# Moving one head's share of the attention output ahead of the block products

## The chip, the cores and the metric

The kernel runs on one core of a Trainium2 chip. Its engines run side by side, each with its own queue of instructions: PE multiplies matrices into PSUM, DVE and ACT do elementwise work (DVE on two tensors, ACT casts, copies and functions), POOL does a little elementwise work and issues some DMAs, SP issues most DMAs. The metric is device time in microseconds from the start to the end of one execution, lower is better.

## The reference

One layer of a decoder trunk on a sequence of 1024 tokens with 1024 features: a mixer of three head groups, then cross-attention into 256 memory tokens, then a gated feed-forward layer. The change is in the cross-attention and its seam to the feed-forward layer. Cut to that:

```python
def cross_attention(hn, mn, w_xq, w_xkv, w_xo):      # 4 heads of 256
    q = (hn @ w_xq).reshape(Bsz, S, N_XHEADS, DH_X)
    k, v = ...                                       # from mn @ w_xkv, 256 memory tokens
    s = jnp.einsum('bshd,bmhd->bhsm', q, k).astype(jnp.float32) * (DH_X ** -0.5)
    p = jax.nn.softmax(s, axis=-1).astype(v.dtype)
    o = jnp.einsum('bhsm,bmhd->bshd', p, v).reshape(Bsz, S, D_MODEL)
    return o @ w_xo

h = h + cross_attention(rmsnorm(h, norm_x_g), rmsnorm(mem, norm_mem_g), w_xq, w_xkv, w_xo)
h = h + conv_glu(rmsnorm(h, norm_ffn_g), w_up, conv_f_w, conv_f_b, w_down)
```

## The kernel before

**Precision.** Every float32 operand is split into a high and a low half (`split`: ACT casts the high half, DVE subtracts it to get the low one), and a product is three matmuls, high x high, high x low and low x high (`mm3`).

**Blocks and order.** The tokens are two blocks of 512, `b` = 0 and 1; the stream lies transposed as `h[b]`, eight tiles `n` of 128 features by 512 tokens. A planner writes out each engine's order from the place of an instruction in the program, with its own estimates of durations; a `high_priority` block sets an earlier place for what stands in it. On the chip each engine follows its written order and waits where an operand is not there yet. Tiles come from pools with a fixed number of places for each tag; a tile waits until a place is free. `big` has six places of 16 KB a partition (tag `b16`). Pools that are opened after others were closed lie on the memory of those, so what is written there waits for the last readers of what lay there.

**Attention.** `q_part` makes q of one block and one half of a head; `scores` multiplies q with the keys in two halves of 256 tokens (`t2`), takes the softmax (DVE maximum, ACT exponential, DVE scaling into `pr`), and leaves a function `turn` in `pending` that transposes `pr` on PE; `catch_up` runs what is pending. After the second half's transposes, ACT and DVE split the result into `pT` (`phi`, `plo`). `o_part` multiplies `pT` with the values.

**Output projection.** Heads 0 to 2 go through a block product: seven products P1 to P7 instead of eight, each of nine matmuls (three 128-row slices, three matmuls each), in four units `ounits[j]` that give the output tiles j and j + 4 of both blocks. Their operands (sums and differences of head outputs) are written to DRAM (`od`), loaded again and split (`part_in`: L1170 load, L1173, L1174). The order of products is P1, P6, P5, P7, P2, P4, P3; each unit needs weight parts A, S, R and Z made from two raw tiles (`prep_a` and so on, L1102, L1103). Head 3 is multiplied plainly by `att_out(b, ...)`, eight tiles of six matmuls, with its weights `w3` (two halves of 512 KB) and its output `o3`, which goes to DRAM (`o3d`) and is loaded again during unit 3. `att_out(0)` stands between unit 3's P4 and its P5, `att_out(1)` behind unit 3.

**Squares.** For the next norm, `keep` stores each finished tile of the stream to DRAM (`hd`, SP), squares it on ACT and sums the squares: two sums on POOL and three squares left alone, five tiles. `rms_tok` multiplies these with a column of ones on PE (tiny matmuls, tile `ssq`, L241: two instructions for each of four token groups and each tile, 40 for five tiles), and `rms_bc` spreads the scale over the partitions, with eight diagonal tiles from DVE (`dg`, L255). The norm is applied by DVE (L1362), after which the feed-forward layer's first products follow (`plain`, L1386).

Of the kernel before, what the change touches and what calls it, by code (L numbers as in the profile page):

```python
# [6 lines left out]
F32 = mybir.dt.float32  # L7
F32R = mybir.dt.float32r
# [109 lines left out]
def trunk(ctx, tc, a, outT, outN):  # L118
# [779 lines left out]
    def scores(b, q, kT):  # L898
        pT = (ap.tile([P, 2, TB], F32R, tag="phi", name="phi"), ap.tile([P, 2, TB], F32R, tag="plo", name="plo"))
        pt = []  # L900
        for t2 in range(2):
            ps = ms_ps("s")
            for i in range(2):
                t = 2 * t2 + i
                for d in range(2):
                    mm3(ps[:, i * NM:(i + 1) * NM], q[d], kT, lambda v: v[:, t * P:(t + 1) * P],
                        lambda v: v[:, d * NM:(d + 1) * NM], d == 0, d == 1)
            catch_up()
            ps3 = ps.rearrange("p (i m) -> p i m", i=2)
            mx = ap.tile([P, 2], F32, tag="mx", name="mx")  # L910
            V.tensor_reduce(out=mx, in_=ps3, axis=AX.X, op=ALU.max)
            V.tensor_tensor(out=mx, in0=mx, in1=rsn[:, 4 * b + 2 * t2:4 * b + 2 * t2 + 2], op=ALU.mult)
            pr = ap.tile([P, 2, NM], F32, tag="pr", name="pr")
            sm = ap.tile([P, 2], F32, tag="sm", name="sm")
            for i in range(2):
                tt = 4 * b + 2 * t2 + i
                A.activation(out=pr[:, i], in_=ps3[:, i], func=AF.Exp, scale=rs2[:, tt:tt + 1], bias=mx[:, i:i + 1],
                             accum_out=sm[:, i:i + 1])
            V.reciprocal(out=sm, in_=sm)
            for i in range(2):  # L920
                V.tensor_scalar(out=pr[:, i], in0=pr[:, i], scalar1=sm[:, i:i + 1], scalar2=None, op0=ALU.mult)

            def turn(t2=t2, pr=pr):
                if t2 == 0:
                    pt.extend([ms_ps("pt0"), ms_ps("pt1")])
                for i in range(2):
                    for m in range(2):
                        t = 2 * t2 + i
                        nc.tensor.transpose(pt[m][:, t * P:(t + 1) * P], pr[:, i, m * P:(m + 1) * P], ident)
                if t2 == 1:  # L930
                    for m in range(2):
                        split(pT[0][:, m], pT[1][:, m], pt[m])

            pending.append(turn)
        return pT

    def att_out(b, Bt, pT, last=None, hook=None):
        for n in range(KT):
            if n in (1, 6):
                catch_up()  # L940
            if n == 2 and hook is not None:
                hook()
            ps = acc_ps("ao")
            for m in range(2):
                mm3(ps, Bt, pT, lambda t: t[:, m, n * P:(n + 1) * P], lambda t: t[:, m, :], m == 0, m == 1)
            resid(b, n, ps)
            if last is not None:
                last(n)
# [2 lines left out]

    NSH = NXH - 1
    od = {p: dram.tile([P, NSH, TB], F32, name=f"od{p}") for p in ORDER}
    o3d = dram.tile([P, NB, 2, TB], F32, name="o3d")

    def o_tile(name, n=4):
        return ap.tile([P, TB], F32, tag=f"o{n}", name=name, bufs=n)
# [1 line left out]
    def o_part(hd, b, v, pT, o):  # L959
        for d in range(2):  # L960
            ps = acc_ps("ov")
            for m in range(2):
                mm3(ps, v, pT, lambda t: t[:, m * NM + d * P:m * NM + (d + 1) * P], lambda t: t[:, m, :], m == 0, m == 1)
            t = o_tile("ot")
            A.copy(out=t, in_=ps)
            o[d, b] = t
            if hd == NSH:
                nc.gpsimd.dma_start(out=o3d[:, b, d], in_=t)
        if hd == NSH:
            return  # L970

        def put(p, t):
            nc.gpsimd.dma_start(out=od[p][:, hd], in_=t)

        if b == 0:
            put("P1", o[0, 0])
            put("P2", o[1, 0])
        else:
            b11, b12, b21, b22 = o[0, 0], o[0, 1], o[1, 0], o[1, 1]
            put("P3", b22)  # L980
            ts = [o_tile(f"t{i}", 2) for i in (1, 2)]
            for out, x, y, p in ((ts[0], b12, b11, "P5"), (ts[1], b22, ts[0], "P6")):
                V.tensor_tensor(out=out, in0=x, in1=y, op=ALU.subtract)
                put(p, out)
            t4 = o_tile("t4", 2)
            V.tensor_tensor(out=t4, in0=b21, in1=ts[1], op=ALU.subtract)
            put("P4", t4)
            t3 = o_tile("t3", 2)
            V.tensor_tensor(out=t3, in0=b22, in1=b12, op=ALU.subtract)
            put("P7", t3)  # L990
# [26 lines left out]
    for b in range(NB):  # L1017
        q_part(0, b, w, nq)
        pT.append(scores(b, q[b], kT))
    kT = st.next()  # L1020
    p3 = [scores(0, nq[0], kT)]
    for b in range(NB):
        o_part(NSH - 1, b, v, pT[b], o)
    v = st.next()
    q_part(1, 0, w, nq)
    catch_up()
    q_part(1, 1, w, nq)
    ox_at = tc.cur_priority
    p3.append(scores(1, nq[1], kT))
    o_part(NSH, 0, v, p3[0], o)  # L1030
    catch_up()
    o_part(NSH, 1, v, p3[1], o)
    hd = [[dram.tile([P, TB], F32, name=f"hd{b}{n}") for n in range(KT)] for b in range(NB)]
    sq3 = [[rsb[:, b]] for b in range(NB)]
# [4 lines left out]
        rms_tok(rs3[:, bs], sq3[b], 4, pool)  # L1039
        pending.append(lambda: rms_bc(rsb[:, b], rs3[:, bs], 4, pool, tag))  # L1040

    def keep(b, acc_tile, new_tile):

        def last(n):
            nc.sync.dma_start(out=hd[b][n], in_=h[b][:, n])
            if n == 1:
                sq3[b].append(acc_tile())
            sq = sq3[b][n] if n < 2 else new_tile()
            A.activation(out=sq, in_=h[b][:, n], func=AF.Square)
            if n >= 5:  # L1050
                sq3[b].append(sq)
            elif n >= 2:
                G.tensor_tensor(out=sq3[b][n % 2], in0=sq3[b][n % 2], in1=sq, op=ALU.add)
        return last

    att.close()
# [7 lines left out]

    fo = ExitStack()
    fp = {tag: fo.enter_context(tc.tile_pool(name=f"f{tag}", bufs=2, reuse_waits="tile"))
          for tag in ("w2", "raw", "s", "u")}
    fp["w1"] = fp["u"]
    fx = fo.enter_context(tc.tile_pool(name="fx", bufs=1, reuse_waits="tile"))
    rs4 = const.tile([P, 4], F32, name="rs4")  # L1070
# [12 lines left out]
    class Unit:  # L1083
# [24 lines left out]

        def prep_s(self):
            r, v = self.raw  # L1110
            s = self.tile("s", 2, 2)
            V.tensor_tensor(out=s[:, 1], in0=v[:, 0], in1=v[:, 1], op=ALU.add)
            V.tensor_tensor(out=s[:, 0], in0=s[:, 1], in1=r[:, 0], op=ALU.subtract)
            self.part("S", s, 2)
            self.s = s

        def prep_r(self):
            r, v = self.raw
            s = self.tile("s", 2, 2)
            V.tensor_tensor(out=s[:, 0], in0=r[:, 0], in1=v[:, 0], op=ALU.subtract)  # L1120
            V.tensor_tensor(out=s[:, 1], in0=r[:, 1], in1=self.s[:, 0], op=ALU.subtract)
            self.part("R", s, 2)
# [78 lines left out]
    def ox_unit(j):  # L1201
# [6 lines left out]
        def take(u, p):  # L1208
# [13 lines left out]
            elif p == "P5":  # L1222
                if "Y" in u.ps and u.u3 is not None:
                    add(1, j + 4, ps)
            elif p == "P2":
                add(0, j, ps)
            elif p == "P4":
                add(0, j + 4, ps)
                add(0, j + 4, u.p1)
            elif p == "P3":  # L1230
                add(1, j, ps)
                add(1, j, u.u2)

        return Unit(fp, f"o{j}", load, take, NSH, 2)

    ounits = [ox_unit(j) for j in range(4)]
    with tc.high_priority(offset=tc.cur_priority - ox_at):
        ounits[0].fetch()
# [2 lines left out]
        ounits[0].prep_r()  # L1241
    ops, xt = {}, {}
    for i, p in enumerate(ORDER):
        if i == 4:

            for x in ("P4", "P3", "P2"):
                xt[x] = fx.tile([P, 2, NSH, HB], F32R, tag=f"x{x}", name=f"o{x}")
        t = xt[p] if i >= 4 else big.tile([P, 2, NSH, HB], F32R, tag="b16", name=f"o{p}")
        ops[p] = t[:, 0], t[:, 1]
        loaded.append(part_in(*ops[p], od[p]))  # L1250
        if i == 3:
            ounits[0].prep_z()
        behind(1)
# [4 lines left out]
    lastw = {}  # L1258

    def get_o3():  # L1260
        t = big.tile([P, 2, NB, 2, TB], F32R, tag="b16", name="o3")
        for b in range(NB):
            loaded.append(part_in(t[:, 0, b], t[:, 1, b], o3d[:, b]))
        lastw["o"] = [(t[:, 0, b], t[:, 1, b]) for b in range(NB)]

    def get_w3():
        t = big.tile([P, 2, 2, D], F32R, tag="b16", name="w3")
# [8 lines left out]
    run(ounits[3], None, ops, dict(P1=get_o3, P6=get_w3, P7=lambda: behind(4), P2=lambda: behind(2),  # L1276
                                   P4=lambda: behind(0)), ("P1", "P6", "P7", "P2", "P4"))
    part_at = tc.cur_priority
    u_spare = lambda: u_tile("sq")
    att_out(0, lastw["w"], lastw["o"][0], keep(0, u_spare, u_spare))  # L1280
    rms_tok(rs3[:, 0:4], sq3[0], 4, fx)
    norm_at = tc.cur_priority
    for p in ("P5", "P3"):
# [114 lines left out]
            rms_bc(rsb[:, 0], rs3[:, 0:4], 4, up, "u", fp["u"])  # L1398

    ops = {}  # L1400
    att_out(1, lastw["w"], lastw["o"][1], keep(1, lambda: u_tile("sq3"), lambda: up.tile([P, HB], F32, tag="t", name="sq", bufs=3)), scale0)
    ops["P1"], ops["P2"] = op_tile("oB11"), op_tile("oB21")
    for q, p in ((0, "P1"), (4, "P2")):
        for k in range(0, 4, 2):
# [299 lines left out]
```

## Time and profile before

| | |
|---|---|
| time, median of 3 runs (lowest to highest) | 1327.38 us (1325.71 to 1328.19) |
| time of the profiled execution | 1325.47 us |
| its span, first to last instruction | 1323.5 us |
| PE busy | 97% of the span |
| DVE, ACT, POOL busy | 72%, 42%, 12% of the span |
| mean granted clock of PE | 0.992 of full speed |

The profile is of one execution. Busy shares are means over all stages; what sets the time of a stage is read from windows of that stage and from the idle time in front of single instructions, for which the profile names what ended it. Matmuls are pipelined: the time that one takes from the engine is the distance between two starts, which is shorter than the duration in its row.

### The profile page before, as it was taken

What the parts mean: (1) busy time and instruction counts of PE and PEld (TensorE: products, weight loads), DVE (VectorE), ACT (ScalarE), POOL (GpSimd) and SP (SyncE); (2) the same over time, 40 slices, a digit from 0 to 9 for tenths busy, and PEclk for the clock granted to TensorE, in tenths of its full rate; (3) what the DMA queues carried; (4) which work ended last, traced back from release to release, by engine and by line L of the source; (5) the groups of instructions that cost most, each with busy time, mean ns of one, the idle gap of its engine ahead of it and who ended that gap; (6) DMA issues with size and microseconds to landing.
All of it is one profiled execution on the core that took longest, in us unless ns stands there. A gap on an engine that the chain in (4) does not pass through costs nothing.

```text
span 1323.5 us, 16301 instructions
## 1 busy us (share of the span) xinstructions
PE 1287.8 (97%) x6192; PEld 1064.6 (80%) x6192; DVE 951.7 (72%) x1454; ACT 559.4 (42%) x867; POOL 153.0 (12%) x155
## 2 busy tenths in 40 slices
PE   8899999999999999899999999999999999999997
PEld 8798788887888878677787888888888887877786
DVE  7958999867754445786789877778776788486424
ACT  6642353647434334533336334333433363353322
POOL 4810011110331011101100000000000001121130
PEclk9999999999999999999799999999999999999999
DMA  8531100112532132733303332223332275776903
GB/s 309 194 115 34 53 24 19 46 49 80 178 93 72 48 104 88 253 105 128 114 14 120 105 118 88 99 101 120 105 102 80 96 285 113 206 219 148 299 18 127
DMA packets 57469, 154.43 MB, mean 117 GB/s; under 512 B 6512, under 2 KB 12272, under 8 KB 55600
## 3 DMA queue, kind: packets, MB, share of 16 engines
q1 hardware_dynamic: 47904, 135.58, 30.1%
q0 software_dynamic: 6608, 14.95, 5.4%
q10 hardware_dynamic: 2880, 2.88, 0.7%
q8 instruction: 48, 0.79, 0.3%
q14 instruction: 29, 0.24, 0.1%
HBM read 110.13 MB, written 43.25 MB: 116 GB/s over the span
## 4 chain that ended last, share of the span: by engine, by line
issue 39%; PE 12%; DMA 3%; DVE 2%; POOL 1%; ACT 1%; POOLq 0%; SPq 0%; DVEq 0%; ACTq 0%
PE Yd L1138 2%; PE Zd L1138 1%; PE Yo L1138 1%; PE Zo L1138 1%; DMA oP<-odP 1%; PE d L214 1%; PE d L212 1%; PE d L213 1%; PE Xd L1138 1%; POOL hd L1488 1%; PE dn L212 1%; PE dn L214 1%; PE dn L213 1%; DMA hd<-c 1%; DMA gt<-gr 1%
## 5 line engine op out<-in xcount | busy, mean ns | idle before, releaser
L1138 PE MATMUL Yu<-oT,w2u 128*128 128x512 f32 x480 | 115.6, 389 | 1.1 <-DVE u L1155 1.1
L1138 PE MATMUL Xu<-oB,w2u 128*128 128x512 f32 x480 | 115.4, 389 | 0.0
L1138 PEld LDWEIGHTS Yu<-oT,w2u 128*128 128x128 f32 x480 | 89.9, 188 | 20.3 <-DVE u L1155 1.5
L1138 PEld LDWEIGHTS Xu<-oB,w2u 128*128 128x128 f32 x480 | 90.1, 188 | 18.7
L99 DVE TENSOR_TENSOR wlo<-raw,whi 128x1024 fp32r<-128x1024 f32 (+2 forms) x57 | 75.4, 1325 | 29.0 <-ACT whi L98 28.3
L98 ACT CAST whi<-raw 128x1024 fp32r<-128x1024 f32 (+1 forms) x55 | 57.5, 1047 | 88.5 <-PE o L213 29.7
L1488 POOL DMA_DIRECT2D hd<-c x32 | 27.4, 900 | 558.6 <-ACT c L1161 453.7
L212 PE MATMUL z<-h1hi,whi 128*128 128x512 f32 x224 | 89.8, 401 | 0.0
L214 PE MATMUL z<-h1hi,wlo 128*128 128x512 f32 x224 | 88.8, 397 | 0.0
L213 PE MATMUL z<-h1lo,whi 128*128 128x512 f32 x224 | 88.7, 396 | 0.0
L1103 DVE TENSOR_TENSOR w2u<-su,w2u 128x1024 fp32r<-128x1024 f32 x40 | 48.9, 1223 | 53.4 <-ACT w2u L1102 53.3
L1102 ACT CAST w2u<-su 128x1024 fp32r<-128x1024 f32 x40 | 42.1, 1053 | 40.4 <-PE Zu L1138 40.2
L1138 PE MATMUL Zu<-oB,w2u 128*128 128x512 f32 x240 | 57.7, 389 | 0.0
L1138 PE MATMUL Yu<-oT,w1u 128*128 128x512 f32 x240 | 57.7, 389 | 0.0
L1138 PE MATMUL Zu<-oT,w2u 128*128 128x512 f32 x240 | 57.6, 389 | 0.0
L1307 DVE SCALAR_TENSOR_TENSOR cv<-gp,cst,cv 128x1024 f32<-128x1024 f32 x44 | 56.5, 1284 | 0.7
L1138 PEld LDWEIGHTS Zu<-oB,w2u 128*128 128x128 f32 x240 | 45.0, 188 | 9.5 <-DVE val L1159 0.2
L1138 PEld LDWEIGHTS Yu<-oT,w1u 128*128 128x128 f32 x240 | 45.0, 188 | 9.5 <-DVE u L1158 0.2
L1138 PEld LDWEIGHTS Zu<-oT,w2u 128*128 128x128 f32 x240 | 45.0, 188 | 9.4
L213 PE MATMUL o<-ylo,whi 128*128 128x512 f32 x128 | 50.3, 394 | 0.0
L212 PE MATMUL o<-yhi,whi 128*128 128x512 f32 x128 | 50.1, 393 | 0.0
L214 PE MATMUL o<-yhi,wlo 128*128 128x512 f32 x128 | 50.0, 392 | 0.0
(459 smaller groups left out, 3227.7 us busy)
## 6 DMA issues: line engine op xcount, KB each, us to landing
rawu<-w_up SPq DMA_DIRECT2D x44, 512.0 KB, 3.5
raw<-w_out SPq DMA_DIRECT2D x16, 512.0 KB, 3.5
rawd<-w_dn SPq DMA_DIRECT2D x16, 512.0 KB, 4.9
hd<-c POOLq DMA_DIRECT2D x32, 256.0 KB, 6.1
raw<-w_in SPq DMA_DIRECT2D x14, 512.0 KB, 3.6
g0P<-gd0P SPq DMA_DIRECT2D x7, 1024.0 KB, 6.7
g1P<-gd1P SPq DMA_DIRECT2D x7, 1024.0 KB, 7.5
oP<-odP SPq DMA_DIRECT2D x7, 768.0 KB, 5.4
```

The source lines that it names most:

```text
L98: eng(out=hi[:, s], in_=raw[:, s])
L99: nc.vector.tensor_tensor(out=lo[:, s], in0=raw[:, s], in1=hi[:, s].bitcast(F32), op=ALU.subtract)
L212: mm(ps, lhsT=ws(w[0]), rhs=xs(x[0]), start=first, stop=False)
L213: mm(ps, lhsT=ws(w[0]), rhs=xs(x[1]), start=False, stop=False)
L214: mm(ps, lhsT=ws(w[1]), rhs=xs(x[0]), start=False, stop=last)
L1102: A.copy(out=t[:, 0], in_=src)
L1103: V.tensor_tensor(out=t[:, 1], in0=src, in1=t[:, 0].bitcast(F32), op=ALU.subtract)
L1138: mm(ps, lhsT=w[:, wi, k * P:(k + 1) * P], rhs=op[xi][:, k], start=first and k == 0 and j == 0, stop=k == n - 1 and j == 2, skip_group_che ...
L1307: V.scalar_tensor_tensor(out=cv, in0=gp[:, k:k + S], scalar=col(C_CFW + 3 * f + k), in1=cv, op0=ALU.mult, op1=ALU.add)
L1488: G.dma_start(out=hd[b][n], in_=t, accum_op=ALU.add)
```

## The change

`att_out(0)` moves from unit 3 to the end of attention, between `scores` of block 1 and block 1's last `o_part`. Its operand is no longer stored and loaded: `o_part` of head 3 and block 0 splits its output into tiles of tag `q`. `w3` is loaded for it into a place of `big`, and a second time during unit 3 for `att_out(1)`. The P2 operand moves to `big`, P7 to the pool `fx`. `o_part` of head 3 and block 0 stands ahead of `scores` of block 1. Block 0's squares are summed while the units finish its tiles: six into one sum, two left alone (three tiles); block 1's are five in one sum and three alone (four tiles). In `scores`, pending transposes run in the first half only, in `att_out` in the middle. Unit 0's weights are placed earlier in the program, `prep_r` of these units writes over its raw tile, and tag `s` has one place instead of two.

```diff
@@ scores
-            catch_up()
+            if t2 == 0:
+                catch_up()
@@ att_out
-            if n in (1, 6):
+            if n == 4:
                 catch_up()
...
-                mm3(ps, Bt, pT, lambda t: t[:, m, n * P:(n + 1) * P], lambda t: t[:, m, :], m == 0, m == 1)
+                mm3(ps, Bt, pT[m], lambda t: t[:, m, n * P:(n + 1) * P], lambda t: t, m == 0, m == 1)
@@ o_part
+            if hd == NSH and b == 0:
+                t = ap.tile([P, 2, TB], F32R, tag="q", name="o3", bufs=6)
+                split(t[:, 0], t[:, 1], ps)
+                o[d, b] = t
+                continue
@@ end of attention
+    o_part(NSH - 1, 0, v, pT[0], o)
     kT = st.next()
     p3 = [scores(0, nq[0], kT)]
-    for b in range(NB):
-        o_part(NSH - 1, b, v, pT[b], o)
+    o_part(NSH - 1, 1, v, pT[1], o)
     v = st.next()
+    w3 = big.tile([P, 2, 2, D], F32R, tag="b16", name="w3")
+    for d in range(2):
+        raw = wst.tile([P, 1056], F32, tag="raw", name="w3r", bufs=2)
+        nc.sync.dma_start(out=raw[:, 0:D], in_=a["w_xo"][d])
+        split(w3[:, 0, d], w3[:, 1, d], raw[:, 0:D])
+    ox_at = tc.cur_priority
     q_part(1, 0, w, nq)
     catch_up()
     q_part(1, 1, w, nq)
-    ox_at = tc.cur_priority
+    o_part(NSH, 0, v, p3[0], o)
     p3.append(scores(1, nq[1], kT))
-    o_part(NSH, 0, v, p3[0], o)
-    catch_up()
+    att_out(0, (w3[:, 0], w3[:, 1]), [(o[d, 0][:, 0], o[d, 0][:, 1]) for d in range(2)])
     o_part(NSH, 1, v, p3[1], o)
@@ keep
-    def keep(b, acc_tile, new_tile):
+    def keep(b, new_tile, lone):
+
+        done = []
 
         def last(n):
             nc.sync.dma_start(out=hd[b][n], in_=h[b][:, n])
-            if n == 1:
-                sq3[b].append(acc_tile())
-            sq = sq3[b][n] if n < 2 else new_tile()
+            sq = new_tile() if done else sq3[b][0]
             A.activation(out=sq, in_=h[b][:, n], func=AF.Square)
-            if n >= 5:
+            if len(done) >= KT - lone:
                 sq3[b].append(sq)
-            elif n >= 2:
-                G.tensor_tensor(out=sq3[b][n % 2], in0=sq3[b][n % 2], in1=sq, op=ALU.add)
+            elif done:
+                G.tensor_tensor(out=sq3[b][0], in0=sq3[b][0], in1=sq, op=ALU.add)
+            done.append(n)
         return last
@@ units
-          for tag in ("w2", "raw", "s", "u")}
+          for tag in ("w2", "s", "raw", "u")}
...
-            s = self.tile("s", 2, 2)
+            s = self.tile("s", 1 if self.nraw == 2 else 2, 2)
...
-            s = self.tile("s", 2, 2)
+            s = r if self.nraw == 2 else self.tile("s", 2, 2)
...
             elif p == "P2":
                 add(0, j, ps)
+                keep0(j)
             elif p == "P4":
                 add(0, j + 4, ps)
                 add(0, j + 4, u.p1)
+                keep0(j + 4)
...
+    keep0 = keep(0, lambda: u_tile("sq"), 2)
...
-        if i == 4:
+        if i == 3:
 
-            for x in ("P4", "P3", "P2"):
+            for x in ("P7", "P4", "P3"):
                 xt[x] = fx.tile([P, 2, NSH, HB], F32R, tag=f"x{x}", name=f"o{x}")
-        t = xt[p] if i >= 4 else big.tile([P, 2, NSH, HB], F32R, tag="b16", name=f"o{p}")
+        t = xt[p] if p in xt else big.tile([P, 2, NSH, HB], F32R, tag="b16", name=f"o{p}")
@@ get_o3: one block instead of two; unit 3
-    att_out(0, lastw["w"], lastw["o"][0], keep(0, u_spare, u_spare))
     rms_tok(rs3[:, 0:4], sq3[0], 4, fx)
...
-    att_out(1, lastw["w"], lastw["o"][1], keep(1, lambda: u_tile("sq3"), lambda: up.tile([P, HB], F32, tag="t", name="sq", bufs=3)), scale0)
+    att_out(1, lastw["w"], lastw["o"], keep(1, lambda: up.tile([P, HB], F32, tag="t", name="sq", bufs=3), 3), scale0)
```

## Rows read from the trace of the kernel before

**Rows 1.** Page, part 1: busy time, share of the span, instructions by engine

```profile
PE 1287.8 (97%) x6192; PEld 1064.6 (80%) x6192; DVE 951.7 (72%) x1454; ACT 559.4 (42%) x867; POOL 153.0 (12%) x155
```

**Rows 2.** What PE waited for over the whole span: total, times, longest

```profile
PE pt L929 <- DVE pr L921: 2.2, 2, 1.8
```

**Rows 3.** Windows: stretch, length, busy time of each engine, PEclk, DMA share, GB/s

```profile
535.00:540.00 5.00, 4.96 (x25) 4.04 (x23) 1.34 (x3) 1.96 (x2) 0.00 (x0) 1.00 0.58 212
540.00:570.00 30.00, 23.89 (x108) 17.74 (x109) 24.14 (x34) 17.27 (x26) 2.14 (x4) 1.00 0.73 271
555.00:560.00 5.00, 3.50 (x14) 2.60 (x15) 4.58 (x6) 3.44 (x4) 0.00 (x0) 1.00 1.01 381
570.00:600.00 30.00, 29.37 (x130) 23.98 (x129) 25.90 (x42) 8.52 (x12) 0.00 (x0) 1.00 0.18 53
600.00:625.00 25.00, 23.63 (x105) 18.54 (x104) 15.73 (x24) 9.13 (x14) 3.79 (x3) 1.00 0.44 154
625.00:660.00 35.00, 32.68 (x154) 27.89 (x154) 25.23 (x40) 13.83 (x18) 5.35 (x5) 0.82 0.31 110
```

**Rows 4.** Timeline of PE in the transition: start, duration, instruction, idle before it

```profile
541.97 0.38 PE L214 MATMUL s<-w,q 128*128 128x256 f32 x1 [0.71 <-DVE q L176]
556.24 0.73 PE L1138 MATMUL Yo<-oP,w2o 128*128 128x512 f32 x2 [2.54 <-ACT w2o L1102]
567.57 1.42 PE L1138 MATMUL Xo<-oP,w2o 128*128 128x512 f32 x5 [1.20 <-DVE w2o L1103]
```

**Rows 5.** Timeline of PE: two block products in a row

```profile
577.46 2.20 PE L1138 MATMUL Yo<-oP,w2o 128*128 128x512 f32 x9
579.50 2.20 PE L1138 MATMUL Xo<-oP,w2o 128*128 128x512 f32 x9
```

**Rows 6.** Page, part 5: the low part's split of a weight tile

```profile
L99 DVE TENSOR_TENSOR wlo<-raw,whi 128x1024 fp32r<-128x1024 f32 (+2 forms) x57 | 75.4, 1325 | 29.0 <-ACT whi L98 28.3
```

**Rows 7.** Timeline of SP: the first of the last three operand loads; the next weights

```profile
552.19 0.33 SPq L1170 DMA_DIRECT2D oP<-odP  x1
561.02 2.09 SPq L1343 DMA_DIRECT2D rawu<-w_up  x3
```

**Rows 8.** The chain that ended last: landing of the last operand load

```profile
553.09 10.26 DMA oP<-odP
```

**Rows 9.** Timeline of DVE: the splits of the last three operands

```profile
558.54 1.76 DVE L1174 TENSOR_TENSOR oP<-oP 128x1536 fp32r<-128x1536 f32 x1 [0.42 <-ACT oP L1173]
561.11 1.76 DVE L1174 TENSOR_TENSOR oP<-oP 128x1536 fp32r<-128x1536 f32 x1 [0.22 <-ACT oP L1173]
564.89 1.76 DVE L1174 TENSOR_TENSOR oP<-oP 128x1536 fp32r<-128x1536 f32 x1 [2.02 <-ACT oP L1173]
```

**Rows 10.** SP's timeline: stores of block 0's stream beside att_out(0)

```profile
617.64 19.61 SPq L1045 DMA_DIRECT2D hd<-h  x9
```

**Rows 11.** Timeline of PE around att_out(0) and the tiny matmuls behind it

```profile
614.09 2.20 PE L1138 MATMUL Yo<-oP,w1o 128*128 128x512 f32 x9
628.06 0.36 PE L241 MATMUL ssq<-ones,rsb 128*128 128x1 f32 x2
629.17 0.36 PE L241 MATMUL ssq<-ones,rsb 128*128 128x1 f32 x2
```

**Rows 12.** Windows of 5 us after the two groups of tiny matmuls

```profile
630.00:635.00 5.00, 5.00 (x18) 4.07 (x19) 0.85 (x2) 0.00 (x0) 1.09 (x2) 0.66 0.00 0
650.00:655.00 5.00, 5.00 (x29) 5.00 (x28) 5.00 (x7) 2.17 (x3) 0.00 (x0) 0.57 0.02 3
655.00:660.00 5.00, 5.00 (x13) 4.03 (x14) 4.97 (x6) 1.16 (x2) 0.00 (x0) 0.50 0.23 57
```

**Rows 13.** Timelines of DVE and POOL in att_out(1): the scale's diagonals, one addition

```profile
641.03 0.87 DVE L255 TENSOR_SCALAR dg<-ident,rh 128x128 fp32r<-128x128 f32 x4
641.82 2.00 DVE L255 TENSOR_SCALAR dg<-ident,rl 128x128 fp32r<-128x128 f32 x4
641.84 1.30 POOL L1053 TENSOR_TENSOR rsb<-rsb,sq 128x512 f32<-128x512 f32 x1 [10.00 <-ACT sq L1049]
```

More of the change, by code (lines that the diff above doesn't have):

```diff
@@ L953, in trunk @@
     od = {p: dram.tile([P, NSH, TB], F32, name=f"od{p}") for p in ORDER}
-    o3d = dram.tile([P, NB, 2, TB], F32, name="o3d")
+    o3d = dram.tile([P, 2, TB], F32, name="o3d")
     def o_tile(name, n=4):
@@ L967, in o_part @@
             if hd == NSH:
-                nc.gpsimd.dma_start(out=o3d[:, b, d], in_=t)
+                nc.gpsimd.dma_start(out=o3d[:, d], in_=t)
         if hd == NSH:
@@ L1260, in get_o3 @@
     def get_o3():
[L1261 to L1264, printed above, removed]
+        t = big.tile([P, 2, 2, TB], F32R, tag="b16", name="o3")
+        loaded.append(part_in(t[:, 0], t[:, 1], o3d))
+        lastw["o"] = [(t[:, 0, d], t[:, 1, d]) for d in range(2)]
     def get_w3():
@@ L1278, in trunk @@
     part_at = tc.cur_priority
-    u_spare = lambda: u_tile("sq")
-    att_out(0, lastw["w"], lastw["o"][0], keep(0, u_spare, u_spare))
     rms_tok(rs3[:, 0:4], sq3[0], 4, fx)
```

## Prediction

> **What bounds the kernel now.** I read the page first: PE is busy 97% of the span, the next engine, DVE, 72% [rows 1]. So time is won only where PE stands still, runs at a lower clock or does less. The view of what PE waited for says where it stands: the longest wait outside the stretch that the change rewrites is that of a transpose for the softmax on DVE, 1.8 us of 2.2 us in two waits [rows 2]. Then I cut the span around the change into windows. The reader is to see how much of each PE is not busy: 6.1 us of the 30 in the transition from attention to the block products (540 to 570), 0.6 us in the next 30, 1.4 us in 600 to 625, and 2.3 us in 625 to 660, where the granted clock is also only 0.82, worth 35 x 0.18 = 6.3 us [rows 3]. Together some 17 us: 1.3% is the most that can be won here without less work. PE's timeline gives the reason inside the transition: it waits for DVE and ACT, which prepare the low half of q and unit 0's and unit 1's weights [rows 4], while DVE is busy 24.1 of the 30 us [rows 3].
>
> **The change, part by part.** The profiled execution took 1325.47 us (its span 1323.5 us and 2 us around it), 1.9 us under the median of 1327.38 us. The sum is made against the former and then set on the median.
>
> (a) *Transposes later.* Inside `scores` the first half's transposes no longer stand ahead of the next work; they go out with the second half's. No instruction is added. What may go are the two waits [rows 2]: between nothing and -2.2 us. I take the longer one, **-1.8**: behind it stand projections that need nothing of the softmax. The places of `pr` (two) still suffice, since both halves are turned before the next `pr` is written.
>
> (b) *`att_out(0)` moved ahead of the units.* One block product of nine matmuls takes 579.50 - 577.46 = 2.04 us, 0.227 us a matmul [rows 5], so the 48 matmuls of `att_out(0)` are 10.9 us. PE's work is the same in sum; it now lies where DVE and ACT are late. New on them: two splits of `w3` in place of none, about 1.3 us of DVE each by the row of L99 [rows 6]; in 535 to 540 DVE is busy 1.3 us of 5 [rows 3], which covers most of it, and without that cover 2.6 us would join the transition. `o3`'s two splits and the eight residual additions are ten instructions; the 34 of before took 24.1 us, 0.71 us each, so ten are 7.1 us (an estimate), in a stretch that PE fills for 23.9 + 10.9 = 34.8 us. DVE would be asked for 31.2 of 34.8 us, 90%; before it was 24.1 in 23.9 us of PE work. The nearest row is 570 to 600, with 25.9 us of DVE against 29.4 us of PE: it lost 0.6 us in 30 [rows 3]. By it 0.7 us of the 6.1 us would be left, a gain of 5.4 us.
>
> Against that stands a new wait. `w3` takes one of the six places of `big`, so the P2 operand gets its place only when the last matmul of `att_out(0)` is done; SP issues in order, so the loads of P4 and P3 and unit 1's weights queue behind P2's, and unit 0's last three products wait for them. Before, these three loads left together at 552.2 us [rows 7], the last landed at 553.1 + 10.3 = 563.4 us [rows 8], and their splits ended at 560.3, 562.9 and 566.7 us [rows 9]: 8.1, 10.7 and 14.5 us after the first left. PE needs them 2.7 (`o_part` of block 1, 12 matmuls) + 8.2 (P1, P6, P5, P7) = 10.9 us after the place is free, then 12.9 and 15.0 us. So they are hidden, by only 0.5 to 2.8 us; 1.4 us is my allowance for P4 and P3, whose places in `fx` can come free only after that `o_part`, 2.7 us later. I take -5.4 + 1.4 = **-4.0**, with the ends -6.1 (every wait gone) and 0 (the waits only change place).
>
> The moved squares and stores: eight stores of block 0's stream leave SP's queue around 620 us, where nine were spread over 19.6 us by their waits for DVE [rows 10], and stand between the weight loads of the units. Each waits for one addition that its product has just triggered, and the next weights are needed a unit (14 us) later: nothing. Two of four `o3d` stores leave POOL's queue, which issues nothing else there: nothing.
>
> (c) *600 to 625.* The second load of `w3` and the one of `o3` were needed at once; now P5, P3 and the tiny matmuls come first, at least 18 x 0.227 = 4.1 us. The 1.4 us of idle time there [rows 3] goes: **-1.4**, ends 0 and -1.4.
>
> (d) *Fewer tiny matmuls.* Ten of them take 629.17 - 628.06 = 1.11 us [rows 11]. Block 0 has three partial sums instead of five, 24 instead of 40 instructions: -1.8 us. Block 1 has four: eight fewer, -0.9 us, or -1.8 us as the clock is halved there. **-2.7**, ends -1.8 (behind block 1's DVE may set the pace) and -3.6.
>
> (e) *The clock.* After the first tiny group the granted clock was 0.66 over 5 us, 1.7 us lost; after the second it sat at 0.57 and 0.50, the lower of the two levels (1.2 GHz) [rows 12]. The first group shrinks by 40% and stands between full products; the second keeps its wait. I take half of the first: **-0.8**, ends 0 and -1.7.
>
> (f) *POOL against DVE.* Block 1's squares are added in one chain, four additions instead of three. Beside one 1.30 us addition four DVE instructions took 2.00 us instead of 0.87 us [rows 13], and these feed the scale that block 0's norm waits for. **+0.6**, ends 0 and +1.1.
>
> Sum: -1.8 - 4.0 - 1.4 - 2.7 - 0.8 + 0.6 = -10.1 us: 1315.4 us on the profiled time, **1317 us** on the median.
>
> The Trainium skill speaks against one part: its page "SBUF — State Buffer", section "Who interferes with whom", says that a VectorE instruction with two SBUF inputs contends with a GpSimd one that reads SBUF, and that the loser is blocked for the whole instruction. The trace agrees that the two can block each other (2.00 against 0.87 us); for additions of two SBUF tensors it shows nothing as clean. By that rule the first of the rivals below would hold.
>
> **The rivals.**
> *DVE stopped in the units.* Five additions of block 0's squares now run on POOL during units 0 to 2, where DVE prepares weights from SBUF. If each stops DVE for its full 1.30 us and nothing absorbs it, +6.5 us: -3.6, 1323.8 us. For it: the slowed row [rows 13], and DVE at 25.9 of 30 us [rows 3]. Against: the 4.1 us that DVE has idle in every 30. Chance 0.08.
> *The transition's waits only move* ((b) = 0): DVE and ACT stay late for unit 0. -6.1, 1321.3 us. For it: DVE and DMA (381 GB/s in 555 to 560) are both near full [rows 3]. Against: 10.9 us more cover. Chance 0.17.
> *Everything is hidden*: all near ends, -15.0, 1312.4 us; with only (b) at its end 1315.2 us. Chance 0.10.
> *The change does not do what it says*: every engine's order is written out afresh and the waits of (a) to (c) come back at other places; only block 0's tiny matmuls are saved, -1.8 us, 1325.6 us, no difference that a measurement of this kernel can tell (0.2%, 2.7 us). For it: the order mixed nine matmuls of a unit into `att_out(0)` before [rows 11], so written positions aren't kept strictly. Chance 0.11.
> *Slower: P2 comes late.* If matmuls of `att_out(0)` are left behind unit 0's first products, each such product takes 2.04 us from the cover of 10.9 us; at four the cover is gone. The three loads would then also share the DMA with the three `w_up` loads, which before came 8.8 us after them [rows 7]: 1.5 MB at 381 GB/s is 4.1 us, so the last split ends 14.5 + 4.1 = 18.6 us after the place is free and unit 0's last three products wait for about 18.6 - 4.1 = 14.5 us in place of 6.1 us: +8.4. A wait like that lets the clock fall as behind the second tiny group, 5 x 0.43 + 5 x 0.50 = 4.7 us [rows 12]. With the rest of the sum (-6.1): +7.0, 1334.4 us. It decides from a wait of about 10 us. Against: no product has to be placed ahead of them. Chance 0.11.
>
> **How the numbers follow.** My forecast has 0.43, with its own range 1314 to 1320. With the rivals: faster 0.43 + 0.08 + 0.17 + 0.10 = 0.78, same 0.11, slower 0.11. Near ends together give 1312.4 us, far ends together (-1.8 + 1.1) 1326.7 us; 1312 to 1326.5 leaves out the slower rival and the edges, under 2 in 10.
>
> **What would show it.** (a) No PE wait on L921 of over 1 us. (b) PE idle under 2.5 us from the end of the q projections to the end of unit 0; if (b) is wrong, its waits name `oP` (the late operand) or DVE's weights. (c) `att_out(1)` starts without a wait. (d) 24 and 32 tiny matmuls. (e) A granted clock above 0.9 after the first group. (f) The second group still waits 1 to 3 us for POOL. The prediction fails if PE shows a wait of many us for P2, or if the time before the products gets shorter and the time behind them longer by as much.

## The result, and the profile after

The changed kernel takes 1313.62 us (median of 4 runs, 1313.06 to 1314.83) against 1327.79 us of the kernel before in the same session (4 runs, 1325.71 to 1330.01): the ratio is 0.9894, 95% interval [0.9877, 0.9912], 14.2 us or 1.06% faster. The forecast was 1317 us in a range of 1312 to 1326.5 us. The profiled execution took 1313.66 us with a span of 1311.6 us, 11.9 us less than the span before: PE was busy 6.6 us less and idle 5.3 us less. Page, part 1, of the changed kernel, which answers to [rows 1]:

```profile
PE 1281.2 (98%) x6168; PEld 1062.6 (81%) x6168; DVE 955.9 (73%) x1457; ACT 560.8 (43%) x868; POOL 156.3 (12%) x156
```

24 matmuls fewer (6168 in place of 6192) are the 16 + 8 tiny ones. What PE waited for from 530 to 690 us, total, times, longest; in the 125 us ahead of that, where [rows 2] stood, this view has no line left:

```profile
PE ssq L241 <- POOL rsb L1064: 1.8, 1, 1.8
PE ao L212 <- DVE h L830: 1.7, 1, 1.7
PE rsb L256 <- DVE dg L255: 1.6, 1, 1.6
PE Yo L1150 <- ACT w2o L1114: 1.4, 1, 1.4
PE Yo L1150 <- DVE u L1230: 1.1, 2, 0.9
PE Yo L1150 <- DVE oP L1186: 0.2, 1, 0.2
```

The windows that answer to [rows 3]:

```profile
540.00:570.00 30.00, 28.05 (x133) 22.76 (x132) 23.38 (x37) 16.79 (x25) 1.08 (x2) 1.00 0.57 210
570.00:600.00 30.00, 27.51 (x118) 21.43 (x117) 27.37 (x41) 10.50 (x15) 4.76 (x3) 1.00 0.37 127
600.00:625.00 25.00, 25.00 (x122) 20.80 (x121) 16.08 (x26) 9.13 (x14) 3.93 (x3) 1.00 0.30 106
625.00:660.00 35.00, 31.55 (x132) 26.30 (x132) 28.50 (x50) 14.05 (x20) 6.62 (x6) 0.85 0.36 120
```

PE has 4.2 us more in 540 to 570, 1.9 us less in the next 30, and all of 600 to 625; the last window no longer holds the same work. Moments on PE's timeline cut the time more fairly: the first `ssq` matmul of the norm ahead of attention (at about 415 us), the end of the last q projection, the end of the last matmul of `att_out(1)`, and the last matmul that spreads block 1's scale (`rsb<-dg`, at 669 us before). In us:

| kernel | to the end of q | to the end of `att_out(1)` | to block 1's scale | rest of the span | timed, ratio to before |
|---|---|---|---|---|---|
| before | 123.7 | 107.8 | 22.5 | 1069.5 | 1 |
| after | 119.9 | 100.1 | 21.9 | 1069.8 | 0.9894 [0.9877, 0.9912] |
| e1_turns_alone | 120.0 | 106.6 | 20.8 | 1074.0 | 0.9959 [0.994, 0.9977] |
| e2_turns_back | 124.0 | 99.8 | 21.9 | 1073.1 | 0.9949 [0.9931, 0.9966] |
| e3_sums_alone | 127.1 | 107.5 | 21.6 | 1070.6 | 1.0008 [0.9985, 1.0031] |
| e8_tiny_again | 119.9 | 104.2 | 20.2 | 1071.6 | 0.9926 [0.9905, 0.9947] |
| e5_adds_on_dve | 119.9 | 99.8 | 18.7 | 1068.4 | 0.9892 [0.987, 0.9915] |
| e6_weights_later | 119.9 | 99.9 | 20.2 | 1069.0 | 0.9888 [0.9868, 0.9908] |
| e7_att_last | 119.9 | 108.1 | 21.9 | 1068.4 | 0.9958 [0.9942, 0.9974] |
| e9_p7_place | 119.9 | 99.8 | 20.2 | 1068.8 | 0.9895 [0.9875, 0.9914] |
| e10_square_on_pool | 119.9 | 102.3 | 20.3 | 1069.4 | 0.9891 [0.9868, 0.9915] |
| e11_p2_own_queue | 119.9 | 106.2 | 18.6 | 1072.7 | 0.9938 [0.9919, 0.9958] |
| e4_two_sums | 119.9 | 99.8 | 21.1 | 1066.3 | 0.9881 [0.9858, 0.9904] |

Of the 11.9 us, 3.85 come ahead of the end of q, 7.8 from there to the end of `att_out(1)` and 0.6 behind it; the rest is 0.3 us longer. The rest differs by up to 8 us between executions whose code there is the same, so a single execution's time settles nothing of 1 or 2 us, but the stretches do.

### The profile page after: what moved, and what is told of

It reads as the page before. It is cut to its first block, busy times and chain, and to the rows that moved or that the text cites. A ratio compares the mean times of both kernels' runs of the same rounds, so it can differ in the third digit from the quotient of the medians.

```text
span 1311.6 us, 16264 instructions
## 1 busy us (share of the span) xinstructions
PE 1281.2 (98%) x6168; PEld 1062.6 (81%) x6168; DVE 955.9 (73%) x1457; ACT 560.8 (43%) x868; POOL 156.3 (12%) x156
## 4 chain that ended last, share of the span: by engine, by line
PE 77%; DVE 8%; issue 6%; DMA 4%; POOL 3%; ACT 1%; SPq 0%; POOLq 0%; DVEq 0%; ACTq 0%
PE Yu L1150 12%; PE Zu L1150 8%; PE Xu L1150 8%; PE z L212 3%; PE z L214 3%; PE z L213 3%; PE Yd L1150 3%; PE q L212 2%; PE q L213 2%; PE q L214 2%; PE o L213 2%; PE o L214 2%; PE o L212 2%; PE Yo L1150 1%; PE Zd L1150 1%
## 5 line engine op out<-in xcount | busy, mean ns | idle before, releaser
L1150 PEld LDWEIGHTS Xu<-oB,w2u 128*128 128x128 f32 x480 | 90.1, 188 | 18.7
L1500 POOL DMA_DIRECT2D hd<-c x32 | 27.4, 896 | 558.0 <-ACT c L1173 453.9
```

What stands on the lines that cost most here:

```text
L1150: mm(ps, lhsT=w[:, wi, k * P:(k + 1) * P], rhs=op[xi][:, k], start=first and k == 0 and j == 0, stop=k == n - 1 and j == 2, skip_group_che ...
L1500: G.dma_start(out=hd[b][n], in_=t, accum_op=ALU.add)
```

## The experiments

**The transposes alone, and the rest alone.** e1_turns_alone is the kernel before with nothing but the edit in `scores` (and `n == 4` in `att_out`):

```diff
-            catch_up()
+            if t2 == 0:
+                catch_up()
```

> The kernel before with one part of the change alone: transposes run later (in scores only in the first half, in att_out at tile 4). Theory, from the two traces: this part is worth more than the 1.8 us forecast, since from the tiny matmuls at 415 us to the end of the q projections the kernel after took 3.9 us less; about -3.5 to -4 us against before, with the wait of PE on DVE's pr gone. Rival (the prediction's own term): -1.8 us. Second rival: this stretch was shortened by the other edits of the change (orders shifted), then 0 here.

e2_turns_back takes the edit in `scores` out of the changed kernel again.

> The kernel after with the transposes of scores put back to run in both halves. Theory: the 3.5 to 4 us come back, ratio to before about 0.992 to 0.993 instead of 0.9894. Rival: the moved att_out(0) and the earlier transposes share a gain, and only 1 to 2 us come back.

Alone it is worth 0.41% [0.23, 0.60], 5.4 us; without it the rest is worth 0.51% [0.34, 0.69], 6.8 us; the two make up 12.2 of the 14.2 us. The stretch to the end of q bears the theory out in both (3.7 and 4.1 us) and neither rival; the times say more than 4 us, e2_turns_back's 0.9949 too, but their intervals are wide enough for it. So the step that was priced at -1.8 us is a third of the gain by the stretch (3.85 of 11.9 us), some 40% by the times. The waits of e2_turns_back from 415 to 545 us, then its window from 415 to 540 and that of the changed kernel (columns as in [rows 3]):

```profile
PE pt L929 <- DVE pr L921: 2.4, 2, 1.9
```

```profile
415.00:540.00 125.00, 122.38 (x646) 103.61 (x645) 61.80 (x128) 49.99 (x111) 12.60 (x22) 1.00 0.27 91
```

```profile
415.00:540.00 125.00, 125.00 (x669) 108.00 (x669) 63.56 (x131) 51.91 (x114) 12.59 (x22) 1.00 0.30 98
```

The waits for `pr` come back with their size in [rows 2], and PE stands still 2.6 us in place of none, yet the stretch is 4.1 us longer with the same matmuls in it. Some 1.5 us of the cost are in no wait that the profile names.

**The sums alone.** e3_sums_alone is the kernel before with the new `keep` and its arguments.

> The kernel before, att_out(0) in its old place, with fewer partial sums alone (three tiles for block 0, four for block 1). Theory: 24 and 32 tiny matmuls instead of 40 and 40 save 1.8 us behind block 0, and as the first group gets shorter the granted clock does not fall behind it (another 1.7 to 2 us); behind block 1 nothing, since there the clock falls earlier; in all -2.5 to -4 us. Rival: the clock stays because of what stands around the group in the kernel after (squares ready earlier, products mixed in), not because of its length; then the clock still falls here and POOL's longer chain of additions (five and four instead of three) delays the group: 0 to -1 us.

The time shows no gain (1.0008). Both expectations were half right: the clock stayed at 1.00 over the 5 us behind the first group, as the theory had it, and POOL's longer chain delayed that group, as the rival had it. Its stretch to the end of `att_out(1)` is 0.4 us shorter, that to the scale 0.8 us, while the stretch ahead of both, where this kernel equals the one before, took 3.4 us longer than there: the waits for `pr` were 4.0 us in this execution, and the granted clock fell behind the second of them. The waits from 415 to 545 us, and two windows:

```profile
PE pt L929 <- DVE pr L921: 4.0, 2, 2.1
```

```profile
510.00:515.00 5.00, 3.22 (x12) 2.62 (x13) 1.93 (x8) 2.25 (x8) 0.00 (x0) 0.76 0.08 30
515.00:520.00 5.00, 5.00 (x30) 4.41 (x29) 1.08 (x2) 0.65 (x2) 0.00 (x0) 0.90 0.00 0
```

So the old order of transposes costs 3.7 us in one execution (before against e1_turns_alone), 4.1 in a second (e2_turns_back against after), 7.1 in a third (e3_sums_alone against e1_turns_alone). And 16 tiny matmuls fewer are worth little where the sums are formed late (0.4 us in the stretch): here PE waited 1.97 us for POOL ahead of the first group, which it did not before.

**The tiny matmuls in their new place.** e8_tiny_again has block 0's group of the changed kernel lengthened from 24 to 40:

```diff
+            for i in range(extra):
+                mm(ps[:, 8 + t:9 + t], lhsT=accs[i][:, t * P:(t + 1) * P], rhs=ones[:, 0:1], start=i == 0,
+                   stop=i == extra - 1)
```

> The kernel after with 16 more tiny matmuls in block 0's group (40 as before, the extra ones into unused columns). Theory that length decides: +1.8 us and the granted clock falls behind the group as before, +1.7 to 2 us more: +3.5 us against after, ratio about 0.992. Rival that the surroundings decide: +1.8 us and the clock stays above 0.95: ratio about 0.9908.

The stretch to the end of `att_out(1)` is 4.3 us longer than in e6_weights_later, which runs the changed kernel's order (below): 1.8 us for the 16 themselves, and the clock, which is down while the group is still running and halved behind it:

```profile
620.00:625.00 5.00, 5.00 (x37) 4.78 (x35) 0.02 (x1) 1.57 (x2) 0.00 (x0) 0.87 0.14 52
625.00:630.00 5.00, 5.00 (x16) 4.23 (x16) 2.29 (x4) 1.85 (x3) 1.03 (x1) 0.50 0.00 0
```

That is 5 x 0.13 + 5 x 0.50 = 3.2 us of lost time, part of which PE's wait for `dg` gives back (0.3 us in place of 1.6). Here, between full products, the 16 cost more than the 2.6 us that (d) and (e) had for block 0. The time alone (0.9926, from 0.9905) would also allow the rival's 0.9908; the rows decide for a fallen clock. That the length decides is not shown by it: in five executions with 24 the clock fell behind the group too (last section), if less, and their stretch stayed at 99.8 us in three.

**Block 1's sums.** e4_two_sums gives block 1 its two sums and five tiles back.

> The changed kernel with block 1's squares summed as before the change: two chains on POOL, three additions, five partial tiles, 40 tiny matmuls in place of 32. By the prediction's terms (eight tiny matmuls 0.9 us, one POOL addition less 0.6 us) it is 0.3 us slower from the end of unit 3 to the next stage's first product. Theory after the runs so far (the granted clock falls in the second tiny group however many there are; the single chain on POOL makes PE wait 1.6 us for dg and 1.8 us for the sum): within 1 us, with the wait for dg back under 1 us. Rival (tiny matmuls at the lower clock cost 0.21 us each): 1.7 us slower.

The stretch to the scale is 21.1 us against 20.2 to 21.9 us in the changed kernel, e6_weights_later and e9_p7_place, whose sums are the changed ones; the time is the same within the interval. So neither the time nor this range tells the three expectations apart. The wait for `dg` is gone here, but this does not show that the two sums did it: behind the first group the clock had fallen (0.66), and e9_p7_place and e11_p2_own_queue, with the changed sums and the same fall, have no wait for `dg` either. What the two sums do change is the time of all eight diagonals, 2.8 us in place of 3.7. And the wait for the sum is as long as before, so the single chain was not its cause (what PE waited for, 630 to 645 us):

```profile
PE ssq L241 <- POOL rsb L1080: 1.8, 1, 1.8
```

**POOL beside DVE.** e5_adds_on_dve moves block 1's four additions to DVE (`(V if b == 1 else G).tensor_tensor(...)`).

> The changed kernel with block 1's additions of squares on DVE in place of POOL; block 0's stay on POOL. Theory (POOL's additions block DVE during the last part of the transition: the group of four dg instructions took 2.92 us beside two POOL additions in place of 0.87): the group is back under 1.2 us, PE's wait for dg (1.6 us) falls below 0.6 us and the second tiny group no longer waits for POOL: 1 to 2 us off the stretch from the last matmul of unit 3 to the first product of the next stage. Rival (DVE is the bound there, not POOL: it is busy 5.00 of 5.00 us): five or six additions more on DVE, 0.7 us each, take back as much as they give, 0 to +2 us.

The timeline of DVE at the scale's diagonals, first the changed kernel, with POOL's two additions from its own timeline, then e5_adds_on_dve:

```profile
629.53 2.92 DVE L255 TENSOR_SCALAR dg<-ident,rh 128x128 fp32r<-128x128 f32 x4
...
629.68 2.69 POOL L1064 TENSOR_TENSOR rsb<-rsb,sq 128x512 f32<-128x512 f32 x2 [1.10 <-ACT sq L1060]
```

```profile
628.36 0.88 DVE L255 TENSOR_SCALAR dg<-ident,rh 128x128 fp32r<-128x128 f32 x4
```

The blocking is real: 2.92 against 0.88 us. PE's wait for `dg` goes, but the clock had fallen behind the first group here too (0.66), and with such a fall that wait is gone in e9_p7_place too. The second group now waits 0.9 us for ACT and 0.6 us for DVE in place of 1.8 us for POOL. The worth in time is not shown: the stretch to the scale is 1.5 us shorter than in e6_weights_later, but e11_p2_own_queue reached the same 18.6 us with its additions on POOL and only a higher clock in the second group, and the time is the same (0.9892 against 0.9888).

**Where the transition still waits.** The next edits tried the causes that the rows name. e6_weights_later puts `ox_at` back behind the last `q_part`.

> The changed kernel with unit 0's weight preparation at its old place in the order, behind the last q projection, in place of ahead of it. Theory (PE's wait of 1.7 us inside att_out(0) for the residual additions comes from DVE preparing unit 0's weights first): the wait goes, 1 to 1.7 us less from the end of the q projections to the end of unit 3. Rival (the weights are then late themselves, as in the kernel before, where PE waited for them): the wait moves to unit 0's first products, 0 to +2 us.

The planner wrote the same order for every engine, so this tested nothing; it is a repetition of the changed kernel, within 0.1% of it, and placing unit 0's weights earlier is an edit of the change that did nothing. The 1.7 us wait for the residual additions (`L830`) stays untested. e9_p7_place exchanges two places in `fx` (`for x in ("P4", "P7", "P3")`).

> The changed kernel with the places of P4 and P7 in fx exchanged, so that P7's load needn't wait for att_out(0)'s tiles and can leave some 6 us earlier. Theory (P7's late load delays its split and those queued behind it on DVE): the PE waits for oP and u of 0.2 to 0.9 us in 565 to 585 go, 0.5 to 2 us less. Rival (DVE is full in 540 to 585 whatever the order, so an earlier P7 split only pushes the other work back): within 0.5 us of the changed kernel, or up to 1 us more as P4 comes later.

No load left earlier, so this did not test P7's load; PE's waits from 540 to 600 us stayed, as did the stretch (99.8 us). e11_p2_own_queue takes P2's load off SP's queue, the order of PE, DVE and ACT unchanged:

```diff
-        loaded.append(part_in(*ops[p], od[p]))
+        loaded.append(part_in(*ops[p], od[p], nc.gpsimd if p == "P2" else nc.sync))
```

> The changed kernel with P2's load issued from POOL's queue, so that the loads of P7, P4 and P3 no longer stand behind it in SP's queue and leave some 6 us earlier; the order of PE, DVE and ACT is the same. Theory (the late loads don't cost: the order of ACT and DVE does): PE's waits between 565 and 580 us stay within 0.4 us of their 2.4 us. Rival (the loads behind P2 are what is late): they fall by 1.5 to 2.4 us.

Both were wrong, and this taught most. SP's timeline shows the other three loads leaving at 556.40 us, where the four of the changed kernel left at 556.22: their own places come free only at the end of `att_out(0)`. And P2's data came later by POOL's queue, so that ACT's cast began at 565.98 in place of 560.61 us. The rows of SP and ACT in the changed kernel, then of SP, ACT and PE in e11_p2_own_queue:

```profile
556.22 3.08 SPq L1182 DMA_DIRECT2D oP<-odP  x4
...
560.61 1.48 ACT L1185 CAST oP<-oP 128x1536 fp32r<-128x1536 f32 x1 [1.07 <-DMA oP<-odP]
```

```profile
556.40 3.04 SPq L1182 DMA_DIRECT2D oP<-odP  x3
...
565.98 1.47 ACT L1185 CAST oP<-oP 128x1536 fp32r<-128x1536 f32 x1 [6.31 <-DMA oP<-odP]
...
568.40 0.50 PE L1150 MATMUL Xo<-oP,w2o 128*128 128x512 f32 x1 [3.46 <-ACT p L1224]
569.29 4.82 PE L1150 MATMUL Xo<-oP,w2o 128*128 128x512 f32 x13 [0.40 <-DVE oP L1186]
```

A cast 5.4 us later made PE stand 3.9 us, and the granted clock was 0.95 over the 30 us behind it (1.5 us); the stretch is 6.3 us longer than in e6_weights_later. So by these two numbers P2's load had some 1.5 us to spare in the changed kernel, and beyond that the slower rival's mechanism is real.

e7_att_last sets `att_out(0)` behind block 1's `o_part`.

> The changed kernel with block 1's o_part (12 matmuls, 2.7 us) ahead of att_out(0) in place of behind it, so the place in big and the places in fx come free up to 2.7 us later against the products that need them. Theory (the late loads of P7, P2, P4 and P3 cost PE time between 565 and 585 us): those waits grow by 1.5 to 2.7 us, and so does the time of the stretch to the end of unit 3. Rival (the loads have slack, or att_out(0)'s 1.7 us wait is what costs and the extra 2.7 us of PE work covers it): 0 to -1.7 us.

The edit moved more than was meant: `att_out(0)` starts 13 us later behind the end of q, and with `catch_up` ahead of `o_part` the last transposes lost their cover. PE's timeline, and SP's loads:

```profile
545.77 0.66 PE L930 MATMUL pt<-ident,pr 128*128 128x128 f32 x2 [4.62 <-DVE pr L922]
550.36 1.22 PE L1151 MATMUL Zo<-oP,w2o 128*128 128x512 f32 x2 [2.79 <-DVE oP L1187]
```

```profile
567.82 2.12 SPq L1183 DMA_DIRECT2D oP<-odP  x4
```

The stretch is 8.2 us longer than in e6_weights_later: these two waits are 7.4 us, and the clock was at 0.50 and 0.56 from 545 to 555 us, against which stand waits of e6_weights_later that are gone here. As a dose for the late loads it says nothing, since other products came ahead of those that need them. It does show what stands uncovered when `att_out(0)` comes later: the last softmax, 4.6 us, and the P5 operand's split behind unit 0's weights, 2.8 us.

e10_square_on_pool computes block 0's first square on POOL, because in the changed kernel ACT stands 3.24 us at it with P4's and P3's casts behind.

> The changed kernel with block 0's first square (unit 0's) computed on POOL in place of ACT. Theory (in the changed kernel ACT stands 3.24 us at this square, which waits for the first residual addition of unit 0, and the casts of P4 and P3 stand behind it; so their splits and unit 1's weights come late): ACT's wait goes, P4's and P3's casts start some 3 us earlier, and PE's waits of 0.87 us (for u) and 1.38 us (for w2o) between 570 and 577 us fall by 1.5 to 2.2 us together. Rival (the late loads themselves set the pace): the casts then wait for the loads, and the PE waits stay within 0.4 us.

Half right. P4's cast did start earlier (565.70 us), but PE's waits between 565 and 580 us did not fall (2.6 us against 2.4). What holds them up, by the rows, is DVE's written order: the residual addition, which waits for PE, stands ahead of the splits, and the two splits then took 4.26 us beside POOL's square in place of 3.5:

```profile
567.28 0.69 DVE L1221 TENSOR_TENSOR h<-h,Xo 128x512 f32<-128x512 f32 x1 [1.95 <-PE Xo L1153]
567.89 4.26 DVE L1189 TENSOR_TENSOR oP<-oP 128x1536 fp32r<-128x1536 f32 x2
```

The stretch is 2.4 us longer than in e6_weights_later, and the square is not the cause of most of it. Behind PE's wait of 1.7 us inside `att_out(0)`, which every engine meets here in the same order as in the changed kernel, the granted clock fell (0.93 from 545 to 550 us, then 0.73), 1.7 us in all; in the changed kernel it stayed at 1.00 behind the same wait:

```profile
550.00:555.00 5.00, 5.00 (x20) 4.04 (x19) 4.97 (x9) 1.91 (x3) 0.00 (x0) 0.73 0.10 39
```

## Why the prediction was right, and where it was mis-sized

The sign, the range and most steps held; the forecast was 3.4 us too slow by the medians, 1.8 us by the profiled executions (a sum of -10.1 against -11.9).

(a) *Transposes: the step that failed in its size.* The mechanism was as said: no wait on `pr` is left. The size was -1.8 us and is -3.85 us by the stretch of the two executions, -5.4 us by time. The step took one wait of one execution for the whole cost. It left out the second wait of [rows 2], a cost of 1.4 us that is no named wait, and that the waits differ between executions: 4.0 us and a fallen clock in e3_sums_alone. Why they differ stays open.

(b) *`att_out(0)` moved.* Forecast -4.0, with ends 0 and -6.1. PE's idle time from the end of q to 600 us fell from 6.8 us to 4.4 us (30.91 - 24.76 + 0.63 before, 33.93 - 31.98 + 2.49 after): -2.3 us, between the forecast and the case of waits that only move. The test that the prediction set, under 2.5 us idle up to the end of unit 0, was not met. But the late operand is only 0.2 us of it: the loads do leave at the end of `att_out(0)`, four of them and not three, since P7 waits too, and P2's has about 1.5 us to spare (forecast for the three: 0.5 to 2.8). The waits are for DVE and ACT: 1.7 us for the residual additions, which DVE's order has behind unit 0's weights, 0.9 and 1.4 us behind a DVE that waited for PE and then had three splits to do. The step reckoned with a DVE busy for 90% of the stretch and 0.7 us of waits. DVE is busy 23.4 of the 30 us from 540 (78%) and 27.4 of the next 30 (91%), and PE waits 4.2 us. The changed kernel's rows of DVE:

```profile
548.28 0.95 DVE L1115 TENSOR_TENSOR w2o<-rawo,w2o 128x768 fp32r<-128x768 f32 x1
549.15 0.15 DVE L913 TENSOR_TENSOR mx<-mx,rsn 128x2 f32<-128x2 f32 x1
549.22 1.27 DVE L830 TENSOR_TENSOR h<-h,ao 128x512 f32<-128x512 f32 x2
...
562.12 1.76 DVE L1186 TENSOR_TENSOR oP<-oP 128x1536 fp32r<-128x1536 f32 x1 [3.48 <-ACT oP L1185]
...
566.88 0.69 DVE L1218 TENSOR_TENSOR h<-h,Xo 128x512 f32<-128x512 f32 x1 [1.94 <-PE Xo L1150]
```

So most of DVE's idle time is 3.5 us in front of P2's operand, which came late, and 1.9 us in front of a product of PE; the work that PE waits for stands behind these in the written order. That the order and not the load sets the waits is argued from such rows: no run changed DVE's order alone.

(c) *600 to 625:* forecast -1.4, found -1.4: the window is full, and the wait for `w3` that stood there before is gone from the list of waits:

```profile
PE ao L212 <- ACT w L175: 1.2, 1, 1.2
```

(d), (e) *Tiny matmuls and clock.* For block 0 forecast -1.8 and -0.8 us. e8_tiny_again gives 4.3 us for 16 tiny matmuls with what their clock costs. In the two executions, 0.08 of 22.6 us (624.3 to 646.9 before) were lost to the clock, 1.8 us, and none after. But (e) and (f) are not two separate terms: in e9_p7_place, where every engine has the changed kernel's order, the clock fell behind the first group (0.66; 0.68 before the change), PE then did not wait for the diagonals, and the stretch is as short (99.8 us). For block 1 forecast -0.9 and found nothing in these two executions: the clock fell at the group's start (0.52 over its 6.65 us), so that 32 took as long as the 40 before (6.67 us). The prediction had allowed for "-1.8 us as the clock is halved there", the wrong way round: the clock fell earlier. Where the clock was higher, the 32 took 3.7 to 4.8 us (e11_p2_own_queue, e9_p7_place and e10_square_on_pool), e4_two_sums' 40 took 5.5 us: the saving is there, and the clock can take it back.

(f) *POOL against DVE:* forecast +0.6, end +1.1. The diagonals lost 2.0 us and PE waited 1.6 us for them in place of 0.8 [rows 13 hold the slowed diagonals of before]: +0.8 us, and the second group waited 1.8 us for POOL, as said; e4_two_sums shows that the longer chain is not what it waits for.

From the end of q on, (b) to (f) make -8.3 us in the forecast and -8.4 us (7.8 + 0.6) in the table. That the sum fits is in part luck, for its terms fit less well: (b) and block 1's part of (d) fell short by 2.6 us, (e) gave 1.0 us more, and some 1.3 us of the gain to the end of `att_out(1)` are in no wait and no clock that the rows show (7.8 less 2.3, 1.4, 1.8, 1.8 and plus 0.8). No run moves `att_out(0)` and leaves the sums as they were, so the parts of (b) to (e) are read from two traces and not separated by a run. The nearest is e8_tiny_again: with a first group as long as before, it keeps 3.6 us (107.8 - 104.2) of this gain.

Of the rivals, DVE stopped in the units did not come: POOL's additions ran from 581 to 608 us for 1.29 to 1.73 us each, and PE waited 0.24 us from 581 to 600 us and nothing from 600 to 625. The Trainium skill's page "SBUF — State Buffer", section "Who interferes with whom", lets whichever of the two issues first keep the ports that they share for its whole instruction and blocks the other. So the prediction's step from it to this rival went too far: it had DVE lose every time, and in the units POOL's additions were slowed too (up to 1.73 us; 1.30 us in [rows 13]). Where DVE had work without slack, the runs agree that it is slowed beside POOL (the diagonals 2.92 against 0.88 us, two splits 4.26 against 3.5); that a block lasts the other's whole instruction is in no row here.

## What to carry to other kernels

A wait read from one execution was a lower bound of what the order cost: where an in-order engine stands behind a softmax with nothing between, the same code lost 3.7 to 7.1 us in three executions. Moving independent matmuls into a stretch where the vector engine is late paid here only in part; by the rows, that engine's written order held its own results back. Look for the instruction at its head that waits for PE. And fewer instructions save their time only where nothing else sets the pace: 16 tiny matmuls were worth 0.4 us beside a late sum, and 4.3 us, clock included, between full products, in one execution each.

## What the runs showed of the hardware that was not expected

The clock behind the tiny matmuls is not settled by their number alone. With 40 in the first group it fell in all three profiled executions (0.58 to 0.68 over the 5 us behind it); with 24 it stayed at 1.00 in five and fell to 0.66 in five, in kernels whose PE order there, e3_sums_alone's aside, is the same; e9_p7_place, where it fell, has the order of the changed kernel on every engine. What decides it stays open. Windows of 5 us behind the first group, first e6_weights_later, then e9_p7_place:

```profile
621.70:626.70 5.00, 5.00 (x23) 4.08 (x24) 4.31 (x7) 2.53 (x3) 1.03 (x1) 1.00 0.31 75
```

```profile
621.50:626.50 5.00, 5.00 (x17) 3.92 (x16) 4.31 (x7) 2.51 (x3) 1.03 (x1) 0.66 0.29 75
```

Of these ten, the second group ran at 0.73 to 0.97 where the clock fell behind the first, at 0.52 to 0.68 where it did not, and both kernels shown need 99.8 to 99.9 and 20.2 us for the two stretches. So the fall cost nothing there: PE would have waited for the diagonals (1.6 us) anyway.

In e11_p2_own_queue a load of 768 KB took 9.0 us from issue to landing by POOL's queue, and the three of the same size by SP's beside it 4.2 to 8.8 us, with a median of 7.1. All four were in flight together, so what the queue alone adds is not shown.
